# A gated attention and convolution block on one core: all attention beside the second half's products, W_out split once, and the scheduler's order for the first half

## Chip, cores and metric

The kernel runs on one core of a Trainium2 chip. The metric is the device time of one execution in microseconds (us); the median of several runs is compared. PE is TensorE (matrix products), PEld its weight loads, ACT ScalarE, DVE VectorE, POOL GpSimd (here it only issues transfers), SP SyncE (the main queue of transfers).

## What is computed

One layer over 2048 tokens of width 1024, in float32:

```python
h = rmsnorm(x, norm_g)
q, k, v, z_att, gb, gc, u, z_conv, g_att, g_conv = split(h @ w_in)   # 6 x 512 ... 2 x 1024 columns
att = chunked_rel_attention(q, k, v, rel_bias)     # 8 heads of 64; own chunk of 64 and 8 before
y_att = (att * silu(z_att)) @ w_att_out
vconv = causal_depthwise_conv(gc * u, conv_w, conv_b)                # width 3
y_conv = (gb * vconv * silu(z_conv)) @ w_conv_out
m = sigmoid(g_att) * y_att + sigmoid(g_conv) * y_conv
out = rmsnorm(x + m @ w_out, final_norm_g)
```

## The kernel before

**Precision.** Each operand of a large product is split into a rounded high part and a low part: ACT copies (rounding), DVE subtracts (split_into for weights, lines 122 and 123; split_pair for tokens, lines 128 and 129). A product is then three matmuls for each 128 of depth: high by high, high by low, low by high (passes, lines 135 to 137).

**Projection.** The tokens go in two halves of 1024. The 48 column tiles of W_in are taken in 24 pairs: 8 gate pairs G, 8 convolution pairs C (two for each block: C and u, B and z_conv), 4 pairs q and k, 2 of v, 2 of z_att. A pair of column tiles by two token blocks of 512 by two halves of the depth is computed with seven products in place of eight (a Strassen-like scheme): ORDER lists them, each has a token operand ops[half, i, j] and a weight operand wops[p, i], and each of them is 12 matmuls into one bank of PSUM. Its evictions (lines 742 to 767) add the seven up, and the pair's own function ev_gate, ev_q and so on finishes and stores to DRAM. The first three pairs of the first half ("plain pairs") are computed directly, from unnormalized tokens.

The loop over seq (line 710) goes through the other pairs: in the first half it builds each weight operand two products ahead (operand; DVE sums, ACT copy, DVE subtraction into a ring of four tiles wr) and stores it to wc_d (line 399); in the second half it loads them back from wc_d, three products ahead (line 381), except for the three plain pairs, whose weights are split there again. At each product of the last first-half pair, operand_steps(1) makes the second half's token operands of the same number i, in the slots that this product frees. The second half's token norms (norm_steps) and the bias tables (reduce_bias) are spread over the first half's products.

**Attention.** A generator that does one stage per call: 4 blocks of 512 queries (c) by 8 heads by 4 groups of 128 queries are 128 units, and 131 stages with the 3 of run-out. A stage holds the scores of one unit (four matmuls, line 190; DVE adds the bias and finds the maximum, ACT the exponential and the scaling), the five transposes of the unit two back (line 210) with their split, and every second time the twelve value matmuls (line 228). POOL's queue loads q, k, v, z and the bias. Blocks c = 0 and 1 need the first half's tokens alone. The score bank ps_s and the transpose bank ps_t have one buffer each. It starts with the last product of the second half's plain pairs, and 64 stages are spread evenly over the 133 products that are left.

**Output stages.** For each half: half_c, 16 items (W_conv_out, then W_att_out, 8 column tiles each) by two token blocks, 12 matmuls each, the weight tile loaded (wraw<-wy) and split an item ahead; then half_d, 16 items of 24 matmuls with the split of W_out (out_weights, lines 834 and 835: 16 tiles, loaded, copied, subtracted), then the residual, the norm and the store. W_out is split in the first half's stage and once more in the second's. pump() spreads the other 67 attention stages over the first half's half_c and half_d.

**What sets the order.** Instructions are written in program order, and a scheduler that plans with its own costs orders each engine's queue ahead of the run: it takes the earliest instruction of the program that is ready in its plan. manual_schedule keeps program order on the engines named. It covers the plain pairs (PE, ACT, DVE), and then, for PE and ACT, the loop up to the last product of the second half's first two pairs. Each engine then runs its queue in order.

Of the kernel before, what the change touches and what calls it, by code (L numbers as in the profile page):

```python
# [17 lines left out]
P = 128  # L18
# [22 lines left out]
def block_kernel(ctx, tc, xb, xt, wp_in, wy, wo, bias, ng, fg, cw, cb, out):  # L41
# [71 lines left out]
    def tick():  # L113
        for it in list(later):
            it[0] -= 1
            if it[0] < 0:
                later.remove(it)
                it[1]()
# [388 lines left out]
    G, C, Q, V, Z = 0, 8, 16, 20, 22  # L507
    conv_gate = lambda *g: [x for b in range(4) for x in (C + 2 * b, C + 2 * b + 1, *g[b:b + 1])]
    order = [[*range(G, G + 4), *conv_gate(G + 4, G + 5, G + 6, G + 7), *range(Q, Q + 8)]]
    order.append([G + 3, G + 4, *range(G, G + PLAIN), *conv_gate(), *range(Q, Q + 8), G + 5, G + 6, G + 7])  # L510
    names = [n * NPAIR + p for n in range(NH) for p in order[n]]
    assert sorted(names) == list(range(2 * NPAIR)) and names[:PLAIN] == list(range(PLAIN))

# [132 lines left out]
    with tc.manual_schedule(engines=engines):  # L646
# [50 lines left out]
        scaled(*held0)  # L697
        for fn in late:
            fn()
    manual = ExitStack()  # L700
    manual.enter_context(tc.manual_schedule(engines=engines - {mybir.EngineType.DVE}))
    x1 = None
    nbias = 0
    att = None
    ab = None
    at_stages = 0
    turned = None
    uv = {}

    for s, (p, i) in enumerate(seq):  # L710
        half = p // NPAIR
        n = names.index(p)
        if half == 0 and i == 1 and n + 1 < NPAIR:
            for k in range(2):
                load_raw(names[n + 1], k)
        elif i == 1 and n in (NPAIR, *range(NPAIR + 2, NPAIR + 1 + PLAIN)):
            for k in range(2):
                load_raw(names[max(n, NPAIR + 1) + 1], k)
        ahead = 3 if half else 2
        while nw < min(len(seq), s + ahead + 1):  # L720
            operand(*seq[nw])
            nw += 1
        if half == 0 and len(built) < 7 and s:
            built.append(next(steps))
        if n == 5 and i == 1:
            for c in range(2):
                for k in range(2):
                    load_x(1, c, k)
            x1 = norm_steps(1)
        if half == 0 and 8 <= n < 22 and i in (2, 5, 4):  # L730
            next(x1, None)
        if half == 0 and 6 <= n < 22 and i in (6, 3) and nbias < 2 * HEADS:
            reduce_bias(nbias // 2, nbias % 2)
            nbias += 1
        ps = dbank("ps_d")
        passes(ps, wops.pop((p, i)), [ops[half, i, j] for j in range(4)])
        tick()
        ev = evs[p % NPAIR]
        g0, g1 = 2 * half, 2 * half + 1
        if i == 1:  # L740
            u = e("u")
            nc.scalar.copy(u, ps)
            uv[p] = [u, None]
        elif i == 2:
            t = e("c11")
            nc.vector.tensor_add(t, uv[p][0], ps)  # L746
            ev[0](g0, 0, t)
        elif i == 6:
            u = uv[p][0]
            nc.vector.tensor_add(u, u, ps)  # L750
        elif i == 5:
            v = uv[p][1] = e("v")
            nc.vector.tensor_add(v, uv[p][0], ps)
        elif i == 7:
            u, v = uv[p]
            t = e("c22")
            nc.vector.tensor_add(t, v, ps)  # L757
            nc.vector.tensor_add(u, u, ps)
            ev[1](g1, 1, t)
        elif i == 4:  # L760
            u = uv[p][0]
            nc.vector.tensor_add(u, u, ps)
            ev[1](g0, 0, u)
        else:
            v = uv.pop(p)[1]
            nc.vector.tensor_add(v, v, ps)
            ev[0](g1, 1, v)
        if n == NPAIR - 1:
            if turned is None:
                for _ in x1:  # L770
                    pass
                turned = operand_steps(1)
            assert next(turned) == i
        elif n == NPAIR + 1 + PLAIN and i == 3:
            first.close()
            att = ExitStack()
            ab = attention(att.enter_context(tc.tile_pool(name="ab", bufs=1, side="right")))
            s0 = s
        elif ab:
            want = (s - s0) * 64 / (len(seq) - s0)  # L780
            while at_stages < min(want, 64):
                next(ab)
                at_stages += 1
        if n == NPAIR + 1 and i == 3:
            manual.close()
        if n == NPAIR + 2 + PLAIN + 8 and i == 1:
            conv_stack.close()
            gp = pool("gp", 5)
        if n == 2 * NPAIR - 1 and i == 5:
            made = make_c(0, ITEMS_C[0])  # L790
            mids = {c: [load_mid(1, b, c) for b in range(4)] for c in (0, 1)}
    while later:
        tick()


    def half_c(hf, mids, made, pump, before):

        cs = (2 * hf, 2 * hf + 1)
        partial = {}
        m = {}  # L800
        att_mids = {}

        for n_, (i, d) in enumerate(ITEMS_C):
            raw, gl = made
            if n_ + 1 < len(ITEMS_C):
                made = make_c(hf, ITEMS_C[n_ + 1])
            w = wtile("wy")
            split_into(w, raw)
            if i == 1 and 3 <= d < 7:
                for c in cs:  # L810
                    att_mids.setdefault(c, []).append(load_mid(0, d - 3, c))
            for n, c in enumerate(cs):
                ps = dbank("ps_d")
                passes(ps, w, mids[c] if i else att_mids[c])
                t = slot("part", F32) if i else gl[n]
                nc.vector.scalar_tensor_tensor(t, gl[n], 1.0, ps, op0=ALU.add, op1=ALU.mult)
                if i:
                    partial[d, c] = t
                else:
                    nc.vector.tensor_add(t, t, partial.pop((d, c)))  # L820
                    m[d, c] = split_pair("m", t)
                pump()
                before(i, d, n)
        return m

    def out_weights(make):

        raw = lambda n: raw_out(n % KT, n // KT)
        nxt = [raw(0), raw(1)]
        for n in range(2 * KT):  # L830
            nxt.append(raw(n + 2) if n + 2 < 2 * KT else None)
            hi, lo = make(n)
            r = nxt.pop(0)
            nc.scalar.copy(hi, r)
            nc.vector.tensor_sub(lo, r, hi.bitcast(F32))
            wout[n % KT, n // KT] = (hi, lo)
            yield
# [5 lines left out]

    wout = {}

    def half_d(hf, m, pump, prepare, at):

        ys = {}
        accs = {}
# [12 lines left out]
        for n, (b, h) in enumerate(items):  # L862
# [3 lines left out]
            ps = dbank("ps_d")  # L866
            c, g = 2 * hf + b // 4, b % 4
            for k in range(KT):
                while (k, h) not in wout:
                    next(prepare)  # L870
                (mh, ml), (wh, wl) = m[k, c], wout[k, h]
                gs = slice(g * P, (g + 1) * P)
                nc.tensor.matmul(ps, lhsT=mh[:, gs], rhs=wh, start=(k == 0), stop=False)  # L873
                nc.tensor.matmul(ps, lhsT=mh[:, gs], rhs=wl, start=False, stop=False)  # L874
                nc.tensor.matmul(ps, lhsT=ml[:, gs], rhs=wh, start=False, stop=(k == KT - 1))  # L875
                if k == 3:
                    pump()
            y = ys[b][h]
            nc.vector.scalar_tensor_tensor(y, ps, 0.25, y, op0=ALU.mult, op1=ALU.add)  # L879
            if h == 0:  # L880
# [4 lines left out]
            if h:  # L885
                r = rsqrt_mean(acc, 1)
                for q, y in enumerate(ys.pop(b)):
                    nc.vector.scalar_tensor_tensor(y, y, r[:, 0:1], fg_sb[q], op0=ALU.mult, op1=ALU.mult)
                    defer(0, lambda q=q, y=y, b=b: nc.sync.dma_start(out[8 * hf + b, :, q * CH:(q + 1) * CH], y))
            pump()  # L890
            if (b, h) == (3, 1):
                for k in range(KT):
                    del m[k, 2 * hf]
        while later:
            tick()
        wout.clear()

    total = NC * HEADS * 4 + BACK

    state = [0, at_stages]  # L900

    def pump():
        state[0] += 1
        want = min(total, 64 + state[0] * (total - 64) / 58)
        while state[1] < want:
            next(ab, None)
            state[1] += 1

    def ring_or_slots(n):
        if 4 <= n < 8:  # L910
            w = wtile("wo")
            return tuple(w[:, s].rearrange("p k c -> p (k c)") for s in range(2))
        return slot("woh"), slot("wol")

    prep = out_weights(ring_or_slots)

    def first_four(i, d, n):
        if i == 0 and d >= 4 and n:
            next(prep)

    m = half_c(0, mids, made, pump, first_four)
    nxt = {}

    def next_half(n):
# [4 lines left out]
            for c in (2, 3):  # L929
                nxt["mids"][c].append(load_mid(1, n - 10, c))  # L930

    half_d(0, m, pump, prep, next_half)
    m.clear()
    for _ in ab:
        pass
    att.close()
    op = pool("op", 24, side="right")
    prep = out_weights(lambda n: tuple(op.tile([P, CH], F32R, tag="wo", name="wo") for s in range(2)) if n < 12 else (slot("woh"), slot("wol")))

    def every_other(i, d, n):  # L940
        if n:
            next(prep, None)

    m = half_c(1, nxt["mids"], nxt["made"], lambda: None, every_other)
    half_d(1, m, lambda: None, prep, lambda n: None)


# [49 lines left out]
```

## Time and profile before

| | |
|---|---|
| median of 3 runs | 1577.24 us (1573.85 to 1580.59) |
| profiled execution | 1571.1 us, span of its trace 1569.3 us |
| mean granted clock of PE | 0.99 |
| busy: PE, DVE, ACT, POOL | 1522.1, 1045.3, 682.6, 154.9 us |
| moved by transfers | 393.65 MB, 251 GB/s in the mean |

The profile is of one execution; durations below are from it. Matmuls are pipelined, and their ends are modelled: what one costs in a stream is the distance between two starts, not its own duration. A line number with an engine names the instruction's line in the kernel; "a<-b" is a tile written from tile b.

### The profile page before, as it was taken

To read this page: it belongs to the slowest core of one execution; us is meant where nothing else is said; L and a number is where in the kernel's file an instruction comes from. 1 tells how busy PE (TensorE), PEld (TensorE's weight loads), DVE (VectorE), ACT (ScalarE), POOL (GpSimd) and SP (SyncE) were. 2 spreads that over 40 slices of the span, in tenths; PEclk is the share of its full clock that TensorE was granted. 3 is DMA by queue.
4 is the path that set the end of the run, shared out by engine and by line. 5 is a ranking of instruction groups with operands and counts; after the bars stand their busy time and mean duration, and the time that the engine had idled before them with its cause. 6 is when DMAs were issued, how large, how long until landed. Compare 5 with 4: busy or idle time off the path is not lost.

```text
span 1569.3 us, 21720 instructions
## 1 busy us (share of the span) xinstructions
PE 1522.1 (97%) x7396; PEld 1268.2 (81%) x7396; DVE 1045.3 (67%) x2094; ACT 682.6 (43%) x1266; POOL 154.9 (10%) x294
## 2 busy tenths in 40 slices
PE   9899999999998999999999999999999999999997
PEld 6677878888786787888888888888887788888886
DVE  7978779797668653666565455446678786656544
ACT  6353343443335242333344444446666676523211
POOL 0000000000000001111121012012332222000000
PEclk9999999999999999999999999999999899999999
DMA  5287898989996926787899889898967668369231
GB/s 210 79 293 298 309 338 306 371 298 311 332 338 230 318 92 215 222 266 238 295 313 314 303 281 287 270 314 274 294 200 228 203 217 273 124 220 316 67 108 68
DMA packets 161711, 393.65 MB, mean 251 GB/s; under 512 B 20160, under 2 KB 40640, under 8 KB 161600
## 3 DMA queue, kind: packets, MB, share of 16 engines
q1 hardware_dynamic: 131392, 306.25, 56.2%
q0 software_dynamic: 20992, 69.22, 14.0%
q10 hardware_dynamic: 9216, 16.78, 2.9%
q8 instruction: 59, 0.97, 0.3%
q14 instruction: 52, 0.43, 0.1%
HBM read 241.18 MB, written 150.99 MB: 250 GB/s over the span
## 4 chain that ended last, share of the span: by engine, by line
PE 62%; DVE 4%; DMA 2%; ACT 1%; issue 1%; SPq 0%; DVEq 0%; ACTq 0%
PE ps_d L137 13%; PE ps_d L135 13%; PE ps_d L136 13%; PE ps_s L190 4%; PE po L228 4%; PE ps_d L873 3%; PE ps_d L875 3%; PE ps_d L874 3%; PE ps_t L210 3%; DMA wraw<-wy 1%; ACT pr L200 1%; DMA wraw<-wo 0%; DVE ps_s L196 0%; DVE ptl L216 0%; PE vt L433 0%
## 5 line engine op out<-in xcount | busy, mean ns | idle before, releaser
L158 POOL DMA_DIRECT2D q<-q x128 | 66.6, 526 | 710.4 <-DVE wc L123 603.3
L200 ACT ACTIVATE pr<-ps_s,nmax 128x640 f32<-128x640 f32 (+4 forms) x128 | 93.3, 729 | 89.8 <-DVE nmax L196 86.2
L196 DVE CUSTOM_DVE_ANT_0 ps_s<-ps_s,bs 128x640 f32<-128x640 f32 (+4 forms) x128 | 95.4, 745 | 48.1 <-PE ps_s L190 47.5
L215 ACT CAST pth<-ps_t 128x640 fp32r<-128x640 f32 (+4 forms) x128 | 79.8, 623 | 99.9 <-PE ps_t L210 98.5
L202 ACT ACTIVATE pr<-pr,rs 128x640 f32<-128x640 f32 (+4 forms) x128 | 97.7, 763 | 24.2 <-DVE rs L201 24.2
L190 PE MATMUL ps_s<-kk,q 128*128 128x320 f32 (+1 forms) x448 | 99.5, 336 | 8.5 <-ACT pr L200 8.3
L122 ACT CAST wc<-wraw 128x512 fp32r<-128x512 f32 x120 | 72.9, 619 | 76.5 <-DMA wc<-wc 41.6
L136 PE MATMUL ps_d<-mid,wy 128*128 128x512 f32 x256 | 101.4, 396 | 0.0
L135 PE MATMUL ps_d<-mid,wy 128*128 128x512 f32 x256 | 101.2, 395 | 0.0
L137 PE MATMUL ps_d<-mid,wy 128*128 128x512 f32 x256 | 101.2, 395 | 0.0
L216 DVE TENSOR_TENSOR ptl<-ps_t,pth 128x640 fp32r<-128x640 f32 (+4 forms) x128 | 94.2, 736 | 1.1 <-ACT pth L215 0.8
L123 DVE TENSOR_TENSOR wc<-wraw,wc 128x512 fp32r<-128x512 f32 x120 | 81.1, 688 | 12.5 <-ACT wc L122 11.5
L210 PE MATMUL ps_t<-ident,pr 128*128 128x128 f32 x560 | 84.2, 276 | 1.0 <-DVE ptl L216 0.8
L228 PE MATMUL po<-pth,vv 128*128 128x256 f32 x336 | 80.1, 272 | 2.3 <-ACT pth L215 2.2
L228 PE MATMUL po<-ptl,vv 128*128 128x256 f32 x336 | 78.5, 281 | 0.0
L190 PEld LDWEIGHTS ps_s<-kk,q 128*128 128x128 f32 x448 | 67.9, 191 | 13.0 <-ACT pr L200 12.3
L210 PEld LDWEIGHTS ps_t<-ident,pr 128*128 128x128 f32 x560 | 63.3, 140 | 11.1 <-issue 3.2
L228 PEld LDWEIGHTS po<-pth,vv 128*128 128x128 f32 x336 | 64.3, 191 | 6.8 <-ACT pth L215 3.4
L228 PEld LDWEIGHTS po<-ptl,vv 128*128 128x128 f32 x336 | 64.5, 192 | 2.7
L757 DVE TENSOR_TENSOR c<-v,ps_d 128x512 f32<-128x512 f32 x45 | 30.9, 687 | 48.7 <-PE ps_d L137 46.4
L884 ACT ACTIVATE sq<-y 128x512 f32<-128x512 f32 x32 | 20.2, 631 | 92.1 <-DVE y L879 92.0
L746 DVE TENSOR_TENSOR c<-u,ps_d 128x512 f32<-128x512 f32 x45 | 30.9, 686 | 42.3 <-PE ps_d L137 38.5
(370 smaller groups left out, 4260.0 us busy)
## 6 DMA issues: line engine op xcount, KB each, us to landing
wc<-wc SPq DMA_DIRECT2D x294, 512.0 KB, 4.7
wraw<-wp_in SPq DMA_DIRECT2D x54, 512.0 KB, 6.2
q<-q POOLq DMA_DIRECT2D x128, 128.0 KB, 4.9
gl<-gate SPq DMA_DIRECT2D x64, 256.0 KB, 3.9
mid<-mid SPq DMA_DIRECT2D x64, 256.0 KB, 5.7
bs<-bias POOLq DMA_DIRECT2D x32, 320.0 KB, 7.1
gate<-c ACTq DMA_DIRECT2D x34, 256.0 KB, 4.6
v<-vst SPq DMA_DIRECT2D x64, 128.0 KB, 4.6
```

The lines of the kernel that those rows point to most:

```text
L123: nc.vector.tensor_sub(w[:, 1], src, w[:, 0].bitcast(F32))
L135: nc.tensor.matmul(ps, lhsT=w[:, 0, k, :], rhs=rh[:, cs], start=(first and k == 0), stop=False)
L136: nc.tensor.matmul(ps, lhsT=w[:, 0, k, :], rhs=rl[:, cs], start=False, stop=False)
L137: nc.tensor.matmul(ps, lhsT=w[:, 1, k, :], rhs=rh[:, cs], start=False, stop=(last and k == len(rhs) - 1))
L190: nc.tensor.matmul(ps[:, i, :m], lhsT=q[s][:, g * P:(g + 1) * P], rhs=kk[:, k1 - n + i * m:k1 - n + (i + 1) * m], start=(s == 0), stop=(s ...
L196: nc.vector.tensor_tensor_reduce(out=view, in0=view, in1=bv, scale=-0.125, scalar=3.0e38, op0=ALU.add, op1=ALU.min, accum_out=nmax)
L200: nc.scalar.activation(out, view, AF.Exp, bias=nmax, scale=-1.0, accum_out=rs)
L202: nc.scalar.activation(pr[:, :n], pr[:, :n], AF.Identity, scale=rs)
L210: nc.tensor.transpose(out=ps[:, j * P:(j + 1) * P], in_=pr[:, j * P:(j + 1) * P], identity=ident)
L215: nc.scalar.copy(hi[:, js, qs], src)
L216: nc.vector.tensor_sub(lo[:, js, qs], src, hi[:, js, qs].bitcast(F32))
L228: nc.tensor.matmul(ps[:, (g0 + a) * P:(g0 + b) * P], lhsT=vv[:, g0 + j, :], rhs=s[:, j, a * P:b * P], start=(i == 0 and s is pt[0]), stop= ...
```

## The change

Four things. The second manual_schedule is dropped, so that the scheduler orders PE and ACT behind the plain pairs. The second half's token operands are made two products later. In the second half the eight pairs q, k, v, z come ahead of the convolution pairs, and all 131 stages of attention are spread over the 133 products. The output stages hold no attention; W_out's split tiles are made once, during the first half_c, in 24 tiles of a pool that takes the attention's place and 8 slots, and serve both half_d.

```diff
-    order.append([G + 3, G + 4, *range(G, G + PLAIN), *conv_gate(), *range(Q, Q + 8), G + 5, G + 6, G + 7])
+    order.append([G + 3, G + 4, *range(G, G + PLAIN), *range(Q, Q + 8), *conv_gate(), G + 5, G + 6, G + 7])
...
-    manual = ExitStack()
-    manual.enter_context(tc.manual_schedule(engines=engines - {mybir.EngineType.DVE}))
+    units = NC * HEADS * 4 + BACK
+    due = []
...
+        if due and due[0] <= s:
+            due.pop(0)
+            next(turned)
...
                 turned = operand_steps(1)
-            assert next(turned) == i
+            due.append(s + 2)
...
-            want = (s - s0) * 64 / (len(seq) - s0)
-            while at_stages < min(want, 64):
+            while at_stages < (s - s0) * units / (len(seq) - s0 - 1):
                 next(ab)
                 at_stages += 1
-        if n == NPAIR + 1 and i == 3:
-            manual.close()
-        if n == NPAIR + 2 + PLAIN + 8 and i == 1:
+        if n == NPAIR + 2 + PLAIN + 16 and i == 1:
             conv_stack.close()
             gp = pool("gp", 5)
...
+    for _ in ab:
+        pass
+    att.close()
+    op = pool("op", 24, side="right")
...
-                while (k, h) not in wout:
-                    next(prepare)
...
-                if k == 3:
-                    pump()
...
-        wout.clear()
...
+    prep = out_weights(lambda n: tuple(op.tile([P, CH], F32R, tag="wo", name="wo") for s in range(2)) if n < 12 else (slot("woh"), slot("wol")))
+    def every_other(i, d, n):
+        if n:
+            next(prep, None)
-    m = half_c(0, mids, made, pump, first_four)
+    m = half_c(0, mids, made, every_other)
...
-    half_d(0, m, pump, prep, next_half)
+    half_d(0, m, next_half)
...
-    m = half_c(1, nxt["mids"], nxt["made"], lambda: None, every_other)
-    half_d(1, m, lambda: None, prep, lambda n: None)
+    m = half_c(1, nxt["mids"], nxt["made"], lambda *a: None)
+    half_d(1, m, lambda n: None)
```

## Rows read from the trace of the kernel before

**Rows 1.** The page's first part: busy us, share of the span, instructions.
```profile
PE 1522.1 (97%) x7396; PEld 1268.2 (81%) x7396; DVE 1045.3 (67%) x2094; ACT 682.6 (43%) x1266; POOL 154.9 (10%) x294
```
**Rows 2.** What PE waited for: us in total, times, longest us.
```profile
PE ps_d L137 <- DVE wc L123: 12.4, 10, 2.9
PE ps_s L190 <- ACT pr L200: 8.3, 5, 3.5
...
PE po L228 <- ACT pth L215: 2.2, 1, 2.2
...
PE ps_t L210 <- DVE ptl L216: 0.8, 2, 0.5
```
**Rows 3.** Stretch, its length, busy PE, PEld, DVE, ACT, POOL; clock, DMA share, GB/s.
```profile
480.00:524.00 44.00, 35.63 (x152) 27.80 (x151) 42.16 (x71) 25.03 (x45) 0.00 (x0) 1.00 0.66 242
524.00:640.00 116.00, 115.11 (x510) 94.57 (x509) 55.88 (x97) 34.93 (x62) 10.76 (x20) 1.00 0.56 189
640.00:1066.70 426.70, 426.68 (x2203) 364.22 (x2202) 239.73 (x491) 180.67 (x350) 66.99 (x126) 1.00 0.86 286
1066.70:1385.60 318.90, 306.74 (x1760) 264.24 (x1760) 227.32 (x515) 204.32 (x368) 76.41 (x143) 0.98 0.68 220
1386.40:1560.00 173.60, 173.60 (x768) 143.79 (x767) 98.90 (x231) 39.67 (x79) 0.00 (x0) 1.00 0.48 161
```
**Rows 4.** PE in order of time, second output stage: start, duration, twelve matmuls apart.
```profile
1386.35 0.39 PE L135 MATMUL ps_d<-mid,wy 128*128 128x512 f32 x1
...
1389.07 0.39 PE L135 MATMUL ps_d<-mid,wy 128*128 128x512 f32 x1
```
**Rows 5.** First output stage, PE busy on lines 190, 210 and 228 alone, in turn.
```profile
1066.70:1385.60 318.90, 55.44 (x256) 0.98 0.68 220
1066.70:1385.60 318.90, 48.29 (x330) 0.98 0.68 220
1066.70:1385.60 318.90, 54.75 (x408) 0.98 0.68 220
```
**Rows 6.** PE in order of time: one whole attention stage (values, transposes, scores).
```profile
1222.68 0.28 PE L228 MATMUL po<-pth,vv 128*128 128x256 f32 x1
...
1224.03 0.73 PE L210 MATMUL ps_t<-ident,pr 128*128 128x128 f32 x5
1224.53 0.83 PE L190 MATMUL ps_s<-kk,q 128*128 128x320 f32 x4
1225.19 0.39 PE L135 MATMUL ps_d<-mid,wy 128*128 128x512 f32 x1
```
**Rows 7.** PE in order of time: two stalls of the first output stage.
```profile
1213.80 0.86 PE L190 MATMUL ps_s<-kk,q 128*128 128x320 f32 x4 [3.33 <-ACT pr L200]
...
1233.10 1.44 PE L190 MATMUL ps_s<-kk,q 128*128 128x320 f32 x4 [3.51 <-ACT pr L200]
```
**Rows 8.** ACT in order of time just before them.
```profile
1212.34 0.62 ACT L122 CAST wy<-wraw 128x512 fp32r<-128x512 f32 x1 [2.19 <-DMA wraw<-wy]
...
1231.64 0.62 ACT L834 CAST wo<-wraw 128x512 fp32r<-128x512 f32 x1 [2.91 <-DMA wraw<-wo]
```
**Rows 9.** PE in order of time: first product behind the plain pairs, first of half two.
```profile
90.97 0.39 PE L135 MATMUL ps_d<-t10h,wc 128*128 128x512 f32 x1
...
523.87 0.39 PE L135 MATMUL ps_d<-t10h,wc 128*128 128x512 f32 x1
```
**Rows 10.** PE in order of time: longest stalls of the first half and its turn.
```profile
221.78 0.67 PE L135 MATMUL ps_d<-t70h,wc 128*128 128x512 f32 x1 [2.43 <-ACT wc L122]
...
513.27 0.50 PE L137 MATMUL ps_d<-t30h,wc 128*128 128x512 f32 x1 [2.94 <-DVE wc L123]
```
**Rows 11.** What ACT waited for from 80 to 480 us.
```profile
ACT wc L122 <- DMA wc<-wc: 41.6, 24, 5.5
...
ACT sz L453 <- DVE c L757: 18.3, 4, 5.4
```
**Rows 12.** Transfers issued from 640 to 1066 us: count, KB each, median us to landing.
```profile
wc<-wc SPq DMA_DIRECT2D x121, 512.0 KB, 4.8
```

More of the change, by code (lines that the diff above doesn't have):

```diff
@@ L793, in block_kernel, with half_c @@
         tick()
-    def half_c(hf, mids, made, pump, before):
+    for _ in ab:
+        pass
+    att.close()
+    op = pool("op", 24, side="right")
+    def half_c(hf, mids, made, before):
         cs = (2 * hf, 2 * hf + 1)
@@ L844, in block_kernel, with half_d @@
     wout = {}
-    def half_d(hf, m, pump, prepare, at):
+    def half_d(hf, m, at):
         ys = {}
@@ L875, in half_d @@
                 nc.tensor.matmul(ps, lhsT=ml[:, gs], rhs=wh, start=False, stop=(k == KT - 1))
-                if k == 3:
-                    pump()
             y = ys[b][h]
@@ L889, in half_d @@
                     defer(0, lambda q=q, y=y, b=b: nc.sync.dma_start(out[8 * hf + b, :, q * CH:(q + 1) * CH], y))
-            pump()
             if (b, h) == (3, 1):
@@ L895, in half_d @@
             tick()
-        wout.clear()
[L898 to L919, printed above, removed]
-    m = half_c(0, mids, made, pump, first_four)
+    prep = out_weights(lambda n: tuple(op.tile([P, CH], F32R, tag="wo", name="wo") for s in range(2)) if n < 12 else (slot("woh"), slot("wol")))
[3 more added lines that the diff above has]
+    m = half_c(0, mids, made, every_other)
     nxt = {}
@@ L930, in next_half @@
                 nxt["mids"][c].append(load_mid(1, n - 10, c))
-    half_d(0, m, pump, prep, next_half)
+    half_d(0, m, next_half)
     m.clear()
[L934 to L942, printed above, removed]
-    m = half_c(1, nxt["mids"], nxt["made"], lambda: None, every_other)
-    half_d(1, m, lambda: None, prep, lambda n: None)
+    m = half_c(1, nxt["mids"], nxt["made"], lambda *a: None)
+    half_d(1, m, lambda n: None)
 def kernel(**inputs):
```

## Prediction

> **What bounds the kernel now.** I read the page's first part, then who TensorE (PE) waits for, then the busy times by stage, and last single stalls in order of time. PE is busy 97% of the span [rows 1]. The span less that busy time is 47 us, and the table of waits names what ended the larger part of it [rows 2]: low halves of weights that VectorE (DVE) makes late (line 123), and softmax work of ScalarE (ACT) and DVE, which exists in the attention alone. So the kernel is bound by PE, and no work of PE is removed: the change can give back stalls, or make new ones.
>
> The table by stage [rows 3] shows where they lie. The third row is the second half's products with the first 64 attention stages: PE 426.68 of 426.70 us. The fourth is the first half's output stage (half_c and half_d) with the other 67: 306.74 of 318.90. The fifth is the second half's output stage with no attention: 173.60 of 173.60.
>
> Busy time hides a part of the loss, so I price stages by pitch. Twelve undisturbed 128x512 matmuls take 1389.07 - 1386.35 = 2.72 us [rows 4], 0.227 us each. That is one product.
>
> **First term: attention leaves the output stage.** After the change this stage has the same 768 matmuls as its twin of the second half, so 173.6 us in place of 318.9 [rows 3]. What leaves it is in [rows 5]: 256 score matmuls (64 units of four), 330 transposes (66 of five), 408 value matmuls (34 groups of twelve). One group of each, undisturbed, is in [rows 6]: values 1224.03 - 1222.68 = 1.35 us, transposes 0.50, scores 0.66. So 34 x 1.35 + 66 x 0.50 + 64 x 0.66 = 121 us of PE go elsewhere; a stage is about 1.83 us. The parts need 173.6 + 121 = 294.7 us, and the stage takes 318.9: it loses 24 us. Idle time alone would say 318.90 - 306.74 = 12.2; the rest is the granted clock, 0.98 in the mean (some 6 us), and gaps too short to be listed. The Trainium skill, Perfetto Trace Analysis, Identifying the Most-Contended Engine, says that matmul busy time is no good measure of how near PE is to its limit, because the instructions are pipelined; by busy time the term would be 12, by pitch 24, and the twin stage's 173.6 us for 768 matmuls agrees with the pitch.
>
> What caused the loss decides how much comes along. The two long stalls of 3.33 and 3.51 us [rows 7] both wait for an exponential on ACT. ACT stood at that time before a weight copy, 2.19 us for wy and 2.91 us for W_out, whose load had not landed [rows 8]; the exponential was queued behind it, and the score bank could not be reused. With the single 2.2 us on the probabilities' copy [rows 2], whose chain also goes back to a late wy, that is 9 of the 12 us. Beside the second half's products this cannot happen after the first three pairs: their weights come ready split from wc_d, straight into the operand tile, with no work of ACT or DVE. What can come along is the other kind, DVE and ACT being merely busy: 8.3 - 6.84 = 1.5 us on scores and 0.8 on transposes [rows 2], 2.3 us for 67 stages.
>
> **Second term: denser attention beside the products.** Now 64 stages lie beside 133 products without one stall; after, 131 do, one to a product. The stretch becomes 426.7 + 121 = 548 us. DVE there: 239.7 + (227.3 - 98.9) = 368 us, 67%. ACT: 180.7 + (204.3 - 39.7) = 345 us, 63%. DMA: 286 GB/s x 426.7 + (220 x 318.9 - 161 x 173.6) makes 164 MB in 548 us, 300 GB/s against 286 now [rows 3]; the weight loads land in 4.8 us [rows 12] and are asked for three products ahead, at least 8.2 us. Nothing is over its limit, but the mix per product is that of the output stage now. I take twice the 2.3 us (131 stages for 67) and double it for what busy time hides: about 9 us, some 6 of them new. Below: 0, as in the third row of [rows 3]. Above: the full loss per stage, 24/65 x 131 = 48 us.
>
> The reordered pairs cost nothing: q, k, v, z of this half are done 56 products after attention starts, and stage 61, the first to load them, comes some five products later, 5 x 4.5 = 23 us, far over a landing of 5 us. Convolution pairs move later by eight pairs; their results are read in the last output stage. POOL's queue carries the same loads as now, one stage per product as in the present output stage, where PE never stood for one of them.
>
> **Third term: W_out once.** Sixteen loads, 16 ACT copies of 0.62 us [rows 8] and 16 DVE subtractions of some 0.7 go from the last output stage. PE is busy all of that stage [rows 3], so it gains nothing; the cover is PE's own 173.6 us. In the first output stage the split stays, its tiles now waiting for the attention's buffers, which end with the last product; the output stage needs W_out some 86 us later (384 x 0.227). The wait may hold ACT for one landing, about 5 us; queued behind is the next wy copy, made one item (5.4 us) ahead. I take 0, bounds 0 and 3 lost.
>
> **Fourth term: the first half.** Its products start at 90.97 and the second half's at 523.87 [rows 9]: 432.9 us. 147 products x 2.72 = 399.8, and 40 transposes of about 0.1 add 4.5, so 28.5 us are lost. Some 9.5 fall at the turn to the second half: 152 matmuls in 44.0 us, where 152 x 0.227 = 34.5 would do [rows 3]. DVE is busy 42.16 of those 44.0 us, and PE waits up to 2.94 us for a low half [rows 10]. The token operands cost DVE 28 subtractions and 12 sums, 40 x 0.6 = 24 us (they start every 0.6 us), and stand ahead of the weights' halves. Two products later means 5.4 us later, into a stretch where DVE works 55.88 of 116 us. Each slot then has been free for two products, so ACT doesn't stand in front of a copy whose slot PE still reads. Their first user is nine products behind the moved start, so nothing becomes late. I expect 6 of 9.5 back; bounds 0 and 9.5.
>
> The other 19 us lie between 91 and 480. ACT keeps program order there: the copy for a product three ahead stands behind the activation of the last product, which waits for a DVE sum (18.3 us for one kind alone), and behind stores that free its slot (41.6 us) [rows 11]; the worst case stopped PE 2.43 us [rows 10]. In the scheduler's order a copy need not queue behind an activation that isn't ready, and so may start a product earlier. Against it: the scheduler plans with landing times of its own, and [rows 8] shows ACT before copies put too early. 42 weight loads and 16 token loads stand in that stretch. The output stage lost 24 us over 32 such copies, at most 0.75 each; if two thirds of that were theirs, 58 x 0.5 = 29 us would be lost. For a gain: the stretch behind the turn, where three pairs of the second half split their weights in the scheduler's order, loses 0.89 us of 116 [rows 3]. I take 5 back, bounds 29 lost and 19 gained.
>
> **Sum.** Back: 24 - 6 = 18 in the middle, 6 at the turn, 5 in the first half: 29 us. The profiled execution takes 1571.1 us (span 1569.3), so 1542; the median of the runs is 6.1 above it, so 1548 in their terms, 1.8% less.
>
> **Rivals.** *Density* (slower): beside products the attention loses per stage what it loses now, 48 us in place of 24, while the first half gives 11: 1577 + 24 - 11 = 1590. It decides when the loss exceeds 0.27 us a stage. For it: the same mix per product as in the output stage. Against: three quarters of the idle there hang on late weight loads, and DVE and ACT stay under 70%. The Trainium skill, Perfetto Trace Analysis, Optimization Strategy, says that interleaving regimes with different limits can improve a kernel; by that rule taking the attention out of the output stage loses. The trace agrees as far as [rows 3] shows the loss where the two are mixed most densely and none where they are mixed thinly. *Scheduler's order costs* (slower): 29 us lost before the turn, nothing gained at it, 18 won later: 1577 + 29 - 18 = 1588; it decides from 18 lost on. *Cancelled*: the first half loses 12 to 20, the rest gains 18: 1571 to 1579. *All comes back*: 24 + 9.5 + 19 = 52 us, 1525.
>
> **How the numbers follow.** Forecast with its own range 1530 to 1567: 0.54. All back: 0.10. Cancelled: 0.14. Density: 0.11. Scheduler's order: 0.11. A range from 1526 to 1586 leaves out about half of the two slower cases and of the best one. About 0.5% (8 us) is what a measurement of this kernel can tell from no change. Faster by more: the forecast, the best case and a little of the cancelled, 0.69. Within: most of the cancelled and parts of the slower ones, 0.15. Slower: 0.16.
>
> **What would show it.** Right: PE busy to within 1% in a stretch of about 550 us with all attention; 174 us for each output stage, both without waits; the second half's first product near 513 us in place of 523.9; no waits on lines 190 or 228 behind a weight copy. Wrong: new idle time of PE on ACT's weight copies (line 122) before 480 us, above all behind a token load; scores waiting for exponentials in the long stretch; weight loads of line 381 landing far over 5 us; or the turn still short of DVE because the scheduler puts the token operands first again.

## The result, and the profile after

Faster by some 1.4%: 1554.25 us in the median (1549.83 to 1560.34, 4 runs) against 1577.55 us (4 runs) of the kernel before on the same chip; ratio 0.9861, 95% interval 0.9823 to 0.99. The profiled execution took 1557.6 us (span 1555.8), 13.5 us less than that of before; the two medians lie 23.3 us apart, because before's profiled execution lies 6.4 us under its median and this one 3.4 us above its own. The sums below are between the two profiles, so they explain 13.5 us; the other 9.8 us are taken up behind the experiments.

The busy times, from the page's first part. Against [rows 1] PE does the same number of instructions, DVE and ACT do 16 fewer each:
```profile
PE 1516.6 (97%) x7396; PEld 1267.9 (81%) x7396; DVE 1039.7 (67%) x2078; ACT 680.1 (44%) x1250; POOL 155.0 (10%) x294
```
What PE waited for; the columns are those of [rows 2]:
```profile
PE ps_p L135 <- DVE c L607: 9.1, 3, 3.6
PE ps_d L137 <- DVE wc L123: 6.0, 4, 3.6
PE ps_d L135 <- ACT wc L122: 3.5, 3, 1.9
PE ps_s L190 <- ACT pr L200: 2.8, 8, 0.6
PE ps_d L135 <- DMA wc<-wc: 2.0, 1, 2.0
PE po L228 <- DMA vv<-v: 1.6, 2, 1.0
```
Scores waited 8.3 us for exponentials in five stalls; now they wait 2.8 us in eight, none over 0.6. The next table has the stretches of the changed kernel, its columns as in [rows 3]: the first half's products without their last 44 us, those 44 us (called the turn below), from there to the first attention stage, the products with attention, and the first output stage:
```profile
93.80:469.80 376.00, 371.96 (x1648) 306.65 (x1647) 293.41 (x524) 147.88 (x268) 0.00 (x0) 1.00 0.91 327
...
469.80:513.80 44.00, 38.49 (x160) 29.89 (x159) 39.64 (x67) 23.24 (x43) 0.00 (x0) 0.96 0.79 279
513.80:615.50 101.70, 99.75 (x433) 82.17 (x432) 53.64 (x83) 33.45 (x55) 7.57 (x14) 0.98 0.50 166
615.50:1198.70 583.20, 577.14 (x3297) 499.80 (x3296) 385.80 (x815) 354.92 (x655) 145.66 (x272) 1.00 0.85 284
1198.70:1372.70 174.00, 174.00 (x769) 144.07 (x768) 96.84 (x218) 40.09 (x80) 1.09 (x2) 1.00 0.58 192
```
The same stretches of before:
```profile
91.00:474.40 383.40, 376.09 (x1654) 306.90 (x1653) 295.83 (x527) 146.09 (x271) 0.00 (x0) 1.00 0.90 325
...
474.40:518.40 44.00, 35.63 (x153) 27.70 (x152) 42.16 (x72) 23.89 (x44) 0.00 (x0) 1.00 0.67 245
...
616.40:1066.70 450.30, 449.39 (x2303) 382.27 (x2302) 251.43 (x519) 187.81 (x366) 70.16 (x132) 1.00 0.85 286
```
The second half's true first product starts at 518.4 us before and 513.8 after. Stretch by stretch, from before to after, in us: plain pairs 91.0 to 93.8 (+2.8; this part is untouched and lies between 90.7 and 93.7 in the runs below), first half 427.4 to 420.0 (-7.4), from there to the attention 98.0 to 101.7 (+3.7), products with attention 450.3 to 583.2 (+132.9), first output stage 319.65 to 174.1 (-145.55), the rest 183 in both. The sum is -13.5.

Below, **loss by pitch** is the sum, over a stretch's matmuls, of the distance to the next start less the median distance for that shape in before. It holds waits and stretches at a lower granted clock alike. Where three losses stand together, they are those of the first half without its last 44 us, of the turn, and from the turn to the attention: 12.6, 10.0 and 0 us before; 6.6, 8.6 and 3.7 us after.

### The profile page after: what moved, and what is told of

It reads as the page before. It is cut to its first block, busy times and chain, and to the rows that moved or that the text cites. A ratio compares the mean times of both kernels' runs of the same rounds, so it can differ in the third digit from the quotient of the medians.

```text
span 1555.8 us, 21590 instructions
## 1 busy us (share of the span) xinstructions
PE 1516.6 (97%) x7396; PEld 1267.9 (81%) x7396; DVE 1039.7 (67%) x2078; ACT 680.1 (44%) x1250; POOL 155.0 (10%) x294
## 4 chain that ended last, share of the span: by engine, by line
PE 83%; DVE 9%; ACT 2%; DMA 2%; issue 2%; POOL 0%; SPq 0%; ACTq 0%; DVEq 0%; POOLq 0%
PE ps_d L137 20%; PE ps_d L135 20%; PE ps_d L136 20%; PE ps_d L876 4%; PE ps_d L874 4%; PE ps_d L875 4%; PE ps_s L190 4%; PE po L228 4%; PE ps_t L210 3%; DVE ptl L216 1%; DVE ps_s L196 1%; DMA wc<-wc 1%; DVE xs L304 1%; ACT pr L200 1%; DMA vv<-v 0%
## 5 line engine op out<-in xcount | busy, mean ns | idle before, releaser
L135 PE MATMUL ps_d<-mid,wy 128*128 128x512 f32 x256 | 99.6, 389 | 0.0
L136 PE MATMUL ps_d<-mid,wy 128*128 128x512 f32 x256 | 99.6, 389 | 0.0
L137 PE MATMUL ps_d<-mid,wy 128*128 128x512 f32 x256 | 99.6, 389 | 0.0
L123 DVE TENSOR_TENSOR wc<-wraw,wc 128x512 fp32r<-128x512 f32 x120 | 82.2, 689 | 13.7 <-ACT wc L122 13.5
L874 PE MATMUL ps_d<-wo,mh 128*128 128x512 f32 x192 | 74.7, 389 | 0.0
L875 PE MATMUL ps_d<-wo,mh 128*128 128x512 f32 x192 | 74.7, 389 | 0.0
L876 PE MATMUL ps_d<-wo,ml 128*128 128x512 f32 x192 | 74.7, 389 | 0.0
L878 DVE SCALAR_TENSOR_TENSOR y<-ps_d,y 128x512 f32<-128x512 f32 x32 | 22.1, 692 | 76.0 <-PE ps_d L876 75.9
```

The lines of the kernel that those rows point to most:

```text
L135: nc.tensor.matmul(ps, lhsT=w[:, 0, k, :], rhs=rh[:, cs], start=(first and k == 0), stop=False)
L136: nc.tensor.matmul(ps, lhsT=w[:, 0, k, :], rhs=rl[:, cs], start=False, stop=False)
L137: nc.tensor.matmul(ps, lhsT=w[:, 1, k, :], rhs=rh[:, cs], start=False, stop=(last and k == len(rhs) - 1))
```

## The experiments

All ratios are to the kernel before on the same chip, with the 95% interval in brackets.

**The parts alone.** In the kernel before, only the second manual_schedule and its close are dropped:

> The kernel before with the scheduler's order behind the plain pairs and nothing else of the change. My theory: the first half's products lose 6 us less by pitch (12.6 before, 6.6 after, 91 to 470 us), the turn and the output stage lose what they lost, so about 6 us faster than before (ratio 0.996). Rival: the order is worth nothing and the first half's gain came from the later operands; then within 2 us of before.

Measured: 1566.45 us, ratio 0.9937 (0.991 to 0.9965). The losses are 5.3, 7.0 and 3.4 us, together 15.7 in place of 22.6.

Next, the kernel before with the token operands two products later and nothing else:

```diff
+    due = []
...
+        if due and due[0] <= s:
+            due.pop(0)
+            next(turned)
...
-            assert next(turned) == i
+            due.append(s + 2)
```


> The kernel before with the token operands two products later and nothing else of the change; program order stays on PE and ACT through the first half. My theory after the first runs (two products are too few to take work from DVE in the turn): the turn's loss stays at 9 to 10 us and the time is that of before, ratio 0.998 to 1.002. Rival (with ACT in program order the delay frees ACT from copies whose slot PE still reads): the turn loses 4 to 6 us less, ratio 0.996 or 0.997.

Measured: 1575.5 us, ratio 0.9998 (0.9976 to 1.0021); the turn lost 14.2 us. That is 4.2 us more than before; by my estimate some 3.5 of them are a lower granted clock (0.92 in the mean of these 44 us in place of 1.00), since PE's waits there add up to 9.1 us against 8.4. The rival fell: two products later are worth nothing in program order. They are worth nothing in the scheduler's order either, which the next run tests: the changed kernel with `next(turned)` in place of `due.append(s + 2)`.

> The changed kernel with the token operands made at once, as before. My theory of the prediction: the turn loses 5 us more, 1559 us in the changed kernel's terms. Rival, from the changed kernel's trace, where DVE is busy 41.4 of the turn's 44 us as before: two products later don't take work from DVE in the turn, and the time is that of the changed kernel within 2 us.

Measured: 1554.31 us, ratio 0.9865 (0.9821 to 0.991), as the changed kernel; losses 6.4, 6.9, 2.7 us. My theory fell, the rival held. (The 41.4 us of DVE that the expectation names were read from 480 to 524 us; in the turn itself it is 39.64, in the table above.)

The changed kernel with `manual` put back and operands at once:

> The attention, pair order and W_out part alone; program order on PE and ACT through the first half and operands at once, as before. My theory: the output stage gives back its 24 us and the denser stretch costs 12, so 12 to 14 us faster than before (ratio 0.992), nothing in the first half. Rival (the first half's order carries the gain): within 4 us of before.

Measured: 1563.46 us, ratio 0.9924 (0.9898 to 0.995). The first half and the turn lost 12.8 and 13.8 us, so nothing was gained there. PE, ACT and DVE run the turn in the same order as before, and PE's four waits there are the same within 0.25 us; the 3.8 us more go with a granted clock of 0.88 in the mean, 1.00 before. The turn, the products with attention and the output stage:
```profile
479.60:523.60 44.00, 35.88 (x134) 27.72 (x133) 39.10 (x66) 22.73 (x41) 0.00 (x0) 0.88 0.64 231
621.50:1204.60 583.10, 576.77 (x3297) 499.79 (x3296) 385.70 (x815) 354.88 (x655) 145.85 (x272) 1.00 0.86 284
1204.60:1378.70 174.10, 174.10 (x769) 144.16 (x769) 96.55 (x218) 39.90 (x80) 1.09 (x2) 1.00 0.58 193
```
The two parts give 0.63% and 0.76%, which add up to the whole change's 1.39%, each known to some 0.3%.

**Which engine's order.** In the kernel before, the engines that keep program order in the loop became PE alone, then ACT alone:

> The kernel before with program order kept on PE through the first half, but not on ACT. My theory (the gain of the scheduler's order is ACT's: weight copies don't queue behind activations that aren't ready): as fast as the kernel with the order dropped on both, ratio 0.994, first half's loss 5 us in place of 12.6. Rival (PE gains by taking a ready matmul of the next product): as before, ratio 1.000.

Measured: 1571.62 us, ratio 0.9978 (0.9958 to 0.9997); losses 7.3, 6.5, 2.6 us.

> The kernel before with program order kept on ACT through the first half, but not on PE. My theory: as before, ratio 0.999 to 1.000, the first half's loss near 12 us. Rival (PE's order is what matters): ratio 0.994.

Measured: 1572.81 us, ratio 0.9974 (0.9959 to 0.9989); losses 10.8, 10.3, 1.7 us.

By the trace the gain up to the attention is ACT's, as my theory has it: 22.8 us are lost with ACT in program order and 16.4 with PE, against 22.6 with both and 15.7 with neither. The whole times don't show it: the two ratios are nearly the same, and 0.9978 is short of the 0.994 expected. In both profiles the first output stage, not edited, took longer, 328.1 and 326.5 us in place of 319.65, by pitch 32.7 and 31.2 us lost in place of 24.2. Its plan is not the reason: PE, ACT and DVE, and the two queues of transfers, run this stage in the same order as in the kernel before, instruction for instruction. What differs is how long ACT stood before copies whose load had not landed. In this stage, in before, then with PE kept, then with ACT kept:
```profile
ACT wy L122 <- DMA wraw<-wy: 7.2, 4, 2.4
ACT wy L122 <- DMA wraw<-wy: 15.0, 6, 4.4
ACT wy L122 <- DMA wraw<-wy: 11.0, 3, 3.9
```
PE's longest stall on scores grew with it, from 3.51 to 6.4 and 5.3 us, and the granted clock of the stage fell from 0.98 to 0.97 in both. The two profiled executions lie 5 us above their kernels' medians, so the same code can lose more or less in this stage by when loads land. How much of it these two kernels lose in the median is not shown.

What ACT waited for in the first half (94 to 470 us) of the changed kernel, to set against [rows 11]:
```profile
ACT wc L122 <- PE ps_d L137: 101.2, 65, 2.1
ACT wc L122 <- DMA wc<-wc: 14.5, 8, 4.0
...
ACT hi L410 <- DVE c L760: 13.8, 3, 7.0
...
ACT xt L293 <- DMA xt<-xt: 6.2, 4, 2.5
```
Its weight copies now mostly stand at the head of the queue and wait for PE to free a slot of the ring of four tiles (101.2 us, 10.1 before). Behind stores they wait 14.5 us in place of 41.6. The feared waits for token loads are there, 6.2 us, and cost PE nothing that the table of its waits shows. The old mechanism is not quite gone: PE's longest wait for a copy before 470 us (1.95 us, at 415 us) stands behind the 7.0 us in which ACT waited for a DVE sum, with three weight copies queued behind.

**The turn.** The changed kernel with the token operands six products later:
```diff
-            due.append(s + 2)
+            due.append(s + 6)
```


> The changed kernel with the token operands six products later in place of two; each is still made five or more products ahead of its first user. If the turn's loss of 8.6 us and the 3.8 behind it come from DVE being given the operands ahead of the weights' low halves: 5 to 9 us faster than the changed kernel. If the scheduler takes DVE's work as it becomes ready, whatever its place in the program, or DVE is simply full: the same within 2 us.

Measured: 1548.13 us (1546.87 to 1548.93), ratio 0.9825 (0.9784 to 0.9865), the fastest kernel here, and under every run of the kernel with operands at once, measured on the same chip (1551.17 to 1557.89). Losses 5.2, 1.5, 1.8 us. The turn and the 44 us behind it:
```profile
458.20:502.20 44.00, 43.43 (x196) 34.91 (x195) 37.67 (x64) 20.59 (x39) 0.00 (x0) 1.00 0.88 310
502.20:546.20 44.00, 42.27 (x187) 34.73 (x186) 30.94 (x50) 19.12 (x33) 0.00 (x0) 1.00 0.75 259
```
DVE is busy 37.67 of the turn's 44 us in place of 39.64, and PE 43.43 in place of 38.49. DVE's busy time alone doesn't decide it: with two products later in program order it was 38.2 us, and 14.2 us were lost. What stands ahead of the weights matters too. In the changed kernel a weight's low half still stood behind token operands. ACT, then DVE, in order of time, just before PE's stall of 3.60 us that ended at 504.37:
```profile
500.65 0.62 ACT L122 CAST wc<-wraw 128x512 fp32r<-128x512 f32 x1 [2.17 <-DMA wc<-wc]
501.18 0.61 ACT L128 CAST t51h<-t 128x512 fp32r<-128x512 f32 x1
...
501.82 0.69 DVE L129 TENSOR_TENSOR t51l<-t,t51h 128x512 fp32r<-128x512 f32 x1 [1.58 <-ACT t51h L128]
502.43 0.69 DVE L360 TENSOR_TENSOR t<-xs 128x512 f32<-128x512 f32 x1
503.03 0.68 DVE L129 TENSOR_TENSOR t52l<-t,t52h 128x512 fp32r<-128x512 f32 x1
503.63 0.69 DVE L123 TENSOR_TENSOR wc<-wraw,wc 128x512 fp32r<-128x512 f32 x1
```
The weight's copy on ACT first waited 2.17 us for a store to free its slot; DVE stood idle for 1.58 us before a token operand whose copy was queued behind it, and then did three token steps ahead of the low half. The products with attention took 587.9 us here and 583.2 in the changed kernel, with all queues in the same order; the granted clock there was 0.99 in place of 1.00. So some 5 us of what the first half gained were lost again in this profile.

**Why the output stage lost 24 us.** First I moved the loads in the kernel before to earlier places in the program, those of W_conv_out and W_att_out three items ahead in place of one, those of W_out three tiles in place of two:

> The kernel before with the output stages' loads of weights issued earlier: W_att_out and W_conv_out three items ahead in place of one, W_out three tiles in place of two. Nothing else is changed. My theory (ACT stands before copies whose load has not landed, with the attention's exponentials behind): the long stalls of 2 to 4 us on scores and values disappear, the first output stage's loss falls from 24 us to about 10, and the kernel is some 10 us faster than before (ratio 0.993). Rival (DVE and ACT are merely too busy there): the stage keeps its length within 3 us.

Measured: 1575.07 us, ratio 0.9973 (0.9947 to 0.9999); the stage took 317.9 us. That looks like the rival, but the lever failed: ACT still stood before a load, now for 7.08 us, and PE 4.78 us for the exponential behind it. SyncE's queue had issued that load late, behind gate loads that waited for a buffer. ACT, then SyncE's queue, in order of time:
```profile
1216.10 0.62 ACT L837 CAST wo<-wraw 128x512 fp32r<-128x512 f32 x1 [7.08 <-DMA wraw<-wo]
...
1194.54 8.46 SPq L544 DMA_DIRECT2D gl<-gate  x3
1203.05 2.32 SPq L844 DMA_DIRECT2D wraw<-wo  x5
```
So I took the loads out. This kernel leaves out the three output weights: a constant is read in their place, by as many copies and subtractions of the same size. The main lines:
```diff
...
-        nc.sync.dma_start(r4, src)
-        return r4
+        return ident[:, None, :].to_broadcast([P, 4, P])
...
-        nc.sync.dma_start(r, wo[k, :, h * CH:(h + 1) * CH])
-        return r
+        return ident[:, None, :].to_broadcast([P, 4, P])
```


> The kernel before without the loads of W_conv_out, W_att_out and W_out in both output stages: ACT copies and DVE subtracts the same sizes from a constant that is always there. All work of ACT, DVE and PE stays, and so does the attention in the first output stage. My theory (ACT stands before copies whose load has not landed): the stalls of 2 to 4 us go, the first output stage's loss falls from 24 us to 8 to 12, the kernel is 12 to 16 us faster than before (ratio 0.991). Rival (DVE and ACT are too busy with two kinds of work): the stage still loses about 20 us and the ratio is 0.997 or more.

Measured: 1556.4 us (1555.52 to 1557.16), ratio 0.9865 (0.9822 to 0.9908). The first output stage, with all its attention, and PE's waits there from 1066 to 1371 us:
```profile
1066.50:1370.80 304.30, 301.37 (x1764) 260.38 (x1764) 228.71 (x518) 206.88 (x374) 76.67 (x143) 1.00 0.62 199
```
```profile
PE ps_s L190 <- ACT pr L200: 1.7, 4, 0.8
PE ps_t L210 <- DVE ptl L216: 1.1, 4, 0.5
```
DVE and ACT work as much as before (227.32 and 204.32 us in [rows 3]), the loss falls from 24.2 to 8.8 us by pitch, and the long stalls are gone. So busy engines are excluded as the main cause. Two things are not apart in this run: some transfers are gone altogether (220 to 199 GB/s), and the scheduler ordered the stage's queues differently (276 of ACT's 368 instructions keep their order). The two runs on the engines' order fill that gap from the other side: there the order stayed, ACT stood longer before loads, and the loss rose to 31 and 33 us.

The kernel before once more, for a second profile:

> The kernel before once more, unchanged, for a second profile. If the stalls of the first output stage depend on when loads land in an execution, its loss differs from the first profile's 24 us by several us, while the first half's losses (12.6 and 10.0 us) repeat within 2; if they are fixed by the plan, all of them repeat.

Measured: 1570.11 us in one execution; losses 10.9 us in the first half, 10.2 in the turn, and 24.5 in the output stage. They repeat: the first expectation fell. Yet both profiles are of executions under the kernel's median. Over all its runs here the kernel before spreads from 1568 to 1589 us; on the chip where the loads were taken out it took 1569.91 to 1584.36 us (7 runs), and without them 1555.52 to 1557.16 (4 runs). That the late loads make much of the spread is likely, not shown. They aren't all of it: of the kernels with no attention in that stage, one spreads over 2 us (six products later), others over 4 to 14 us in 4 to 7 runs.

**Density.** The changed kernel with the token operands six products later, and attention packed more densely from the 60th product on:
```diff
-            while at_stages < (s - s0) * units / (len(seq) - s0 - 1):
+            while at_stages < min(units, s - s0 + max(0, s - s0 - 60) / 2):
```


> The changed kernel with operands six products later and denser attention: one stage per product for 60 products, then three stages for two products, so that it is done some 25 products before the end. If density costs, as the density rival has it: the dense stretch loses clearly more per stage than the 0.1 to 0.2 us of the changed kernel, 10 us or more slower than the variant with six products alone (1548 us). If there is room left on ACT and DVE: within 4 us of it.

Measured: 1559.26 us (1554.9 to 1569.2), ratio 0.9892 (0.9852 to 0.9931), 11 us over the variant with six products alone. Its products with attention took 593.3 us in place of 587.9, but 3.26 us of that is one wait for a load of v that began at 724 us, where the density is the same. The same wait takes 3.3 us in the run with operands at once and 1.0 in the changed kernel, although both run this stretch in the same order, so density isn't its cause. The two profiles lie 10.4 us apart, and another 3.0 of these lie in the plain pairs, which nobody edited. Some 2 us are left for the denser stretch and 1.9 us for a longer output stage; what density costs this run doesn't settle.

Last, on top of six products later, the scaling of the probabilities on POOL in place of ACT:

```diff
-            nc.scalar.activation(pr[:, :n], pr[:, :n], AF.Identity, scale=rs)
+            nc.gpsimd.tensor_scalar(pr[:, :n], pr[:, :n], rs[:, 0:1], None, op0=ALU.mult)
```


> The changed kernel with operands six products later, and the scaling of the probabilities (line 202, 0.76 us of ACT in each of 128 units) on POOL in place of ACT. If the long stretch's remaining 12 us are scores waiting for a busy ACT: 3 to 8 us faster than the variant with six products alone (1548 us), unless POOL is slow at it; if POOL needs more than 2 us for one, or the attention's loads queue behind it, slower.

Measured: 1556.38 us, ratio 0.9869 (0.9817 to 0.992), 8 us slower than without it; the products with attention took 591.0 us in place of 587.9. Duration on POOL in ns, least, median, most:
```profile
L202 POOL TENSOR_SCALAR pr<-pr,rs x128: 597/1884/2196, 605.2 to 1180.6; 128x640 f32<-128x640 f32 x96, 128x128 f32<-128x128 f32 x8, 128x256 f32<-128x256 f32 x8, 128x384 f32<-128x384 f32 x8
```
One scaling takes some 1.9 us on POOL, 0.76 on ACT, and transposes now wait for POOL (5.4 us in all). So this does not tell whether a freer ACT would help.

## Why the prediction was right

1554.25 us lies in the range, 6 us above the forecast of 1548; 29 us were forecast, and 23 came between the medians. The terms of the sum were worked out in the profiles' time, and there 13.5 of the 29 came. So the forecast was nearer than its terms: the 9.8 us between the two figures are no term of it, and that part was luck. Where they may lie the runs with one engine's order show: the stage that the change relieves loses 24 us in before's two profiles, which lie under its median, and 31 to 33 us in two longer executions (of kernels edited only ahead of it), with the same order of instructions.

- *Attention leaves the output stage*: 24 of 24 us. The stage takes 174.1 us. Taking the loads away removed 15.4 us of the loss, so weight loads that land late, ahead of exponentials on ACT, are the larger part of its cause; 8.8 us stay without them.
- *Denser attention*: mis-sized. 132.9 - 121 = 12 us in place of 6; 8.9 of them lie behind product matmuls (372.2 us for 1584 of them, 363.3 before), in short waits of scores, values and transposes. Net 12.6 in place of 18. The density rival's 0.37 us a stage did not come: 12 us over 131 stages is 0.09. The prediction set the rule on interleaving of the Trainium skill (Perfetto Trace Analysis, Optimization Strategy) beside that rival and said that the trace agrees; it does not, since the loss lay where the two were interleaved in the output stage. Nor does a run here test the rule: attention is interleaved with matrix products in every kernel, and with its loads gone the output stage lost 8.8 us with 67 stages, against 13.7 by pitch for 131 beside the products.
- *W_out once*: nothing, as taken; PE runs both output stages without a wait.
- *The first half*: my row for the second half's start was its third product (the second pair's first), so 5.4 us of the 28.5 were no loss; 22.6 were. 6.0 of 12.6 came back between 91 and 470 us, where I took 5, and by the mechanism named, ACT's order.
- *The turn*: failed. I took 6 us back from operands two products later; alone they give nothing, with either order. The scheduler's order by itself took the turn from 10.0 to 7.0 us (6.9 with operands at once in the changed kernel); with two products later it was 8.6, at a granted clock of 0.96, and 3.7 us were lost behind it. PE did wait for low halves that DVE made late, as the step says. It was wrong that 5.4 us of delay would clear them, and that DVE's fullness was all: six products cleared the turn, with DVE hardly less busy. Of the signs of being wrong, this one came (token operands ahead of the weights), and small waits of scores in the long stretch (2.8 us).

## What to carry to other kernels

On an engine that runs its queue in order, a copy that waits for a load holds up all work queued behind it. Keep such copies away from short-lived work: put work with tight buffers beside products whose operands need no copy. Judge such a stage by the pitch of its matmuls, since idle time showed half of its loss.

At a hand-over between stages, look at what stands ahead of the urgent work in each queue, and move what isn't urgent far enough: two products gave nothing here, six cleared the turn; other distances were not tried.

Program order on two engines cost nearly as much as the restructuring gave (0.63% against 0.76%). Test the parts of a change alone, and read each from its own stretch. Take more than one profile of a stage that waits for loads: with the same order of instructions it differed by up to 8.5 us.

## What was not expected

The unedited output stage took 319.65, 328.1 and 326.5 us in three kernels that differ only ahead of it and run it in the same order. Executions of the kernel before spread over 20 us, those without the loads of the output weights over 2. The granted clock moved the turn by some 4 us (0.88 in place of 1.00) with the same instructions and the same waits.
